# First pass of a one-core encoder block: more weight tiles between an operation and its use, open stage borders, plain fp32 for two of three query weights

## The chip, the cores and the metric

The kernel runs on one core of a Trainium2 chip. The metric is the device time of one execution in microseconds (us). Before the change its median is 3540.93 us over 3 runs (3540.81 to 3542.72). All times below are in us unless marked ns.

## The reference

One layer over 512 tokens of width 2048, in float32:

```
h    = rms_norm(x) * g1
q, k, v, f, pin, gates = split(h @ w_in)            # w_in: 2048 x 8200
attn = forgetting attention (8 heads of 128, causal, logits + cumsum(log_sigmoid(f)))
pool = (trailing means over 2/4/8/16 tokens - pin) @ w_groups * scale
y    = sig(g_a) * (attn @ w_branch_attn) + sig(g_p) * (pool @ w_branch_pool)
x    = x + y @ w_out
q2   = rms_norm(x) * g2 @ w_query                   # 8 heads x 256
idx, gate = top 16 of (q2a . keys1) + (q2b . keys2) per head, softmax
x    = x + sum_k gelu(xn . expert_u[idx]) * gate * expert_v[idx]
```

## The kernel before

The first 128 tokens (block A) go through the layer alone, in a **first pass**. The other 384 tokens follow in a second pass, and the experts after that. The change touches the first pass, and the point where the second begins.

**Weight tiles.** The first pass multiplies 112 weight tiles of 128 x 2048 (1 MB each), in the order of the list `plan` (L112 to L115): 0 to 63 for the projection (16 groups of 4: pin, pin, q, k, v, g, g, q, k, v, then six g), 64 to 79 for the branch projections, 80 to 95 for the output projection (wo), 96 to 111 for the query weights (wqu). "Tile 17" below is the one at place 17. Four tiles in a row make one 512-column result in PSUM.

**Two ways to use a tile.** A *split* tile is cut into two fp32r parts in two halves: ScalarE (ACT) casts the high part (`whi`, L162), VectorE (DVE) subtracts for the low part (`wlo`, L174), and TensorE (PE) does three matmuls for each of four k blocks. A *plain* tile (`None` in the plan) is used as it was loaded, in full fp32, four matmuls. Before the change every third tile is plain (place n with n % 3 == 2). Loads are issued by the SP queue (L152) into 3 buffers `wraw`, with a fourth (`xraw`) until near the end of the branch projections. A buffer comes free when the second `wlo` has read it, or for a plain tile when PE has multiplied it. `next_w`, `ahead` and `after` (L184 to L196) decide how far the loads and splits are issued ahead: some two tiles.

**Side work.** Everything else (pooling, head norms, attention of block A, the merge, the norm, the scores) is written as generators. In the middle of each tile's matmuls (L238) `run_gens` lets every live generator go on to its next `yield`, so one `yield` is one tile. What a generator issues to PE stands in PE's queue in the middle of that tile, and PE works through its queue in order, as every engine does. `qkA_norm` scales and squares four heads on ACT, takes a reciprocal root by Ln and Exp (L318, L319), multiplies on DVE (L478) and, one tile later, transposes on PE (L482). `attendA` does scores, softmax (L515 to L519), transposes (L523) and the product with v (L529). `mergedA` transposes the merged result (L591) and splits it, `normedA` does this for the new x (L657). `inputs_b` prepares the second pass's input: for each of 8 chunks it loads `xB` (L628) into one of two buffers, scales it (L636), casts (L638) and subtracts (`hl`, L640). The load of chunk c+1 stands in SP's queue right after the `hl` that frees its buffer was issued, among the loads of the weight tiles.

**Borders.** Before the branch projections all generators are run to their end (L571), before the output projection two rounds of them are run (L611), and after the query weights all of them (L880), which includes the retrieval's top 16 (`topk16`) of the last heads. Then the second pass starts with tile 112 and on.

Of the kernel before, what the change touches and what calls it, by code (L numbers as in the profile page):

```python
# [62 lines left out]
def block_kernel(ctx, tc, a):  # L63
# [48 lines left out]
    plan = [(a["w1A"][col1[kind] + i, q], "dve") for kind, i in groups_a for q in range(4)]  # L112
    for name in ("wbrA", "woA", "wquA"):
        plan += [(a[name][i, q], "dve") for i in range(4) for q in range(4)]
    plan = [(ap, None if n % 3 == 2 else eng) for n, (ap, eng) in enumerate(plan)]  # L115
    plan += [(a[src1[kind]][i], "dve") for kind, i in order_b]
    for name in ("wbr", "wo", "wqu"):
        plan += [(a[name][i], "dve") for i in range(KD)]
# [9 lines left out]
    cnt = [0]  # L128
# [3 lines left out]
    raws, his, parts = {}, {}, {}  # L132
# [33 lines left out]
    def ensure_split(n):  # L166

        ensure_hi(n)
        while st["split"] < min(n + 1, st["hi"]):
# [9 lines left out]
            else:  # L179
                parts[i] = (hi, lo)  # L180

    def next_w():
        n = st["use"]
        st["use"] += 1  # L184
        ensure_split(cnt[n + 1] - 1)
        ensure_load(n + (2 if extra["raws"] is None else 3))
        ensure_split(cnt[n] + 3)
        return parts.pop(n) if plan[n][1] else raws.pop(n)

    def ahead():  # L190
        n = st["use"]
        ensure_hi(cnt[n] + (2 if plan[n - 1][1] else 3))

    def after():
        n = st["use"]
        ensure_split(cnt[n] + (2 if plan[n - 1][1] else 3))  # L196

    gens = []

# [182 lines left out]
    def poolA(c, ps):  # L382
        t = rowsA(ps, "raw", 3)
        yield
        pm, pc = bank(), bank()
        for j in range(4):
            nc.tensor.matmul(pm[:, j * P:(j + 1) * P], lhsT=t[:, j * P:(j + 1) * P],
                             rhs=bands[:, 2 * c + j // 2, :], start=True, stop=True)
        for j in range(4):
            nc.tensor.matmul(pc[:, j * 16:(j + 1) * 16], lhsT=t[:, j * P:(j + 1) * P],  # L390
                             rhs=ident[:, P - 16:], start=True, stop=True)
        m = p1.tile([P, 4, NA], F32, name="mx", bufs=2)
        nc.scalar.copy(m.rearrange("p j t -> p (j t)"), pm)
        nc.scalar.copy(carry[:, 4 * c:4 * c + 4, :].rearrange("p j t -> p (j t)"), pc[:, :64])
        yield
        pg = bank()
        for gg in range(2):
            for dt in range(2):
                for kc in range(2):
                    o = (4 * c + 2 * gg + kc) * 256 + dt * P  # L400
                    i = 2 * gg + dt
                    nc.tensor.matmul(pg[:, i * P:(i + 1) * P], lhsT=wpgA[:, o:o + P],
                                     rhs=m[:, 2 * gg + kc, :], start=kc == 0, stop=kc == 1)
        for j in range(4):
            i = 4 * c + j
            nc.scalar.activation(ap32[:, 8 + i, :], pg[:, j * P:(j + 1) * P], AF.Copy,
                                 scale=psc[:, i:i + 1])
        split_to(ap32, aph, apl, 8 + 4 * c)
# [25 lines left out]
    def forgetA():  # L434
        yield
        ps = bank()
        for k in range(KD):
            nc.tensor.matmul(ps[:, :H], lhsT=xA[:, k, :], rhs=fraw[:, k * H:(k + 1) * H],
                             start=k == 0, stop=k == KD - 1)
        fl = p1.tile([P, H], F32, name="fr")  # L440
        nc.scalar.activation(fl, ps[:, :H], AF.Copy, scale=rsn[:, 0:1])
        yield
        pt = bank()
        nc.tensor.transpose(pt[:H, :NA], fl, ident)
        log_forget(p1, pt, NA, 0, ccA, 0.0, ("fz", "fe", "fu", "fl"))
        yield
        yield
        pt = bank()
        nc.tensor.transpose(pt[:, :H], ccA, ident[:H, :H])
        nc.scalar.copy(cT[:, 0, :], pt[:, :H])  # L450
# [17 lines left out]
    def qkA_norm(which, hb, ps):  # L468
        t = rowsA(ps, "raw", 3)
        v = p1.tile([P, 12], F32, name="hv", bufs=2)  # L470
        sq = p1.tile([P, S], F32, name="sqA")
        for j in range(4):
            nc.scalar.activation(sq[:, j * P:(j + 1) * P], t[:, j * P:(j + 1) * P], AF.Square,
                                 accum_out=v[:, j:j + 1])
        nc.vector.tensor_scalar(v[:, :4], v[:, :4], 1.0 / P, EPS, op0=OP.mult, op1=OP.add)
        rsqrt_nr(v[:, 4:8], v[:, :4], v[:, 8:])
        yield
        nc.vector.tensor_tensor(quad(t), quad(t), v[:, 4:8, None].to_broadcast([P, 4, P]), op=OP.mult)  # L478
        yield
        pt = bank()  # L480
        for j in range(4):
            nc.tensor.transpose(pt[:, j * P:(j + 1) * P], t[:, j * P:(j + 1) * P], ident)  # L482
        out = p1.tile([P, 4, NA], F32, name="n%d" % which)
        nc.scalar.activation(out.rearrange("p j t -> p (j t)"), pt, AF.Copy,
                             scale=(kg if which else qg)[:, 0:1])
        qkA[which, hb] = out
        if which:
            nc.scalar.dma_start(kA_d[hb], out)

    def attendA(hb, ps):  # L490
# [4 lines left out]
        for j in range(4):  # L495
            h = 4 * hb + j
            nc.sync.dma_start(ck[:, j, :], c_d[h:h + 1, :NA].to_broadcast([P, NA]))
        yield
        yield
        qn, kn = qkA.pop((0, hb)), qkA.pop((1, hb))  # L500
        pss = bank()
        for j in range(4):
# [15 lines left out]
        nc.vector.reciprocal(sm[:, :, 1:2], sm[:, :, 1:2])  # L518
        nc.vector.tensor_tensor(pr, pr, sm[:, :, 1:2].to_broadcast([P, 4, NA]), op=OP.mult)  # L519
        yield  # L520
        pt = bank()
        for j in range(4):
            nc.tensor.transpose(pt[:, j * P:(j + 1) * P], pr[:, j, :], ident)  # L523
        PT = p1.tile([P, 4, NA], F32, name="PT")
        nc.scalar.copy(PT.rearrange("p j t -> p (j t)"), pt)
        yield
        pa = bank()
        for j in range(4):
# [18 lines left out]
    for n, (kind, i) in enumerate(groups_a):  # L547
# [20 lines left out]
        after()  # L568
        if n == 9:
            gens.append(rest_rstd())  # L570
    for g in list(gens):  # L571
        for _ in g:
            pass
    gens.clear()
    es_1.close()


    mAh = pA.tile([P, KD, NA], F32R, name="XH")
    mAl = pA.tile([P, KD, NA], F32R, name="XL")
# [5 lines left out]
        yield  # L585

    def mergedA(i, ga):
        yield
        tb = bank()
        for j in range(4):  # L590
            nc.tensor.transpose(tb[:, j * P:(j + 1) * P], ga[:, j * P:(j + 1) * P], ident)  # L591
        nc.scalar.copy(m32[:, 4 * i:4 * i + 4, :].rearrange("p j t -> p (j t)"), tb)
        split_to(m32, mAh, mAl, 4 * i)

    for i in range(4):
# [12 lines left out]
        nc.vector.tensor_tensor(ga, ga, gb, op=OP.add)  # L608
        after()
        gens.append(mergedA(i, ga))  # L610
    for _ in range(2):  # L611
        run_gens()
    es_z.close()


# [6 lines left out]
    def inputs_b():  # L622
        rb = row_bcast(p2, [rsn[:, b:b + 1] for b in range(1, NTB)], "rstdB")
        xs = {}

        def load(c):
            xs[c] = p2.tile([P, 2, NB], F32, name="xB", bufs=2)
            nc.sync.dma_start(xs[c].rearrange("p j t -> p (j t)"), a["xB"][c])  # L628

        load(0)  # L630
        for c in range(KD // 2):
            if c + 1 < KD // 2:
                load(c + 1)
            for j in range(2):
                k = 2 * c + j
                nc.vector.scalar_tensor_tensor(xs[c][:, j, :], xs[c][:, j, :], g1[:, k:k + 1], rb,  # L636
                                               op0=OP.mult, op1=OP.mult)
                nc.scalar.copy(hh[:, k, :], xs[c][:, j, :])  # L638
                yield
                nc.vector.tensor_tensor(hl[:, k, :], xs[c][:, j, :], hh[:, k, :].bitcast(F32),  # L640
                                        op=OP.subtract)


    gens.append(inputs_b())
    nAh = pA.tile([P, KD, NA], F32R, name="YH")
# [5 lines left out]
    def normedA(i):  # L651
        xs = xr0[:, i * S:(i + 1) * S]
        nc.scalar.dma_start(x2t_d[:, i * S:(i + 1) * S], xs)
        yield
        tb = bank()
        for j in range(4):
            nc.tensor.transpose(tb[:, j * P:(j + 1) * P], xs[:, j * P:(j + 1) * P], ident)  # L657
        nc.vector.tensor_tensor(n32[:, 4 * i:4 * i + 4, :], quad(tb),
                                g2[:, 4 * i:4 * i + 4, None].to_broadcast([P, 4, NA]), op=OP.mult)
        split_to(n32, nAh, nAl, 4 * i)  # L660
        yield
        t = p3.tile([P, S], F32, name="scr", bufs=2)
        nc.scalar.activation(t, xs, AF.Square, accum_out=ssA[:, i:i + 1])

    for i in range(4):
        ps = acc_bank()
        for q in range(4):
            mmA(ps, m32, mAh, mAl, 4 * q, q == 0, q == 3, run_gens)
            ahead()
            if q < 3:  # L670
                after()
        xs = xr0[:, i * S:(i + 1) * S]
        nc.vector.tensor_tensor(xs, xs, ps, op=OP.add)
        after()
# [173 lines left out]
    def scores_a(c, ps, kk):  # L848
# [15 lines left out]
        s = pk.tile([P, 4, P], F32, name="s4", bufs=2)  # L864
        nc.scalar.activation(s.rearrange("p j t -> p (j t)"), pss, AF.Copy, scale=rstA[:, 0:1])
        yield
        for j in range(2):
            yield from blkA.job(2 * c + j, (s[:, 2 * j, :], s[:, 2 * j + 1, :]))

    for i in range(4):  # L870
        kk = p3.tile([P, 2, 2 * P], F32, name="kk", bufs=2)
        nc.scalar.dma_start(kk, a["keys"][2 * i:2 * i + 2].rearrange("h p i k -> p h (i k)"))
# [4 lines left out]
            after()  # L877
        gens.append(scores_a(i, ps, kk))
        run_gens_last()
    while gens:  # L880
        run_gens()

    es_y = [None]

    def start_rows():
        yield from tok_u(x2t_d, rstA[:, 0:1])
        for _ in blkA.decode():
            yield
# [685 lines left out]
```

## Time and profile before

| what | value |
|---|---|
| median of 3 runs | 3540.93 us |
| profiled execution | 3543.57 us |
| its span (first to last instruction) | 3541.8 us |
| PE busy over the span | 3353.7 us, 95% |
| DVE busy | 2699.1 us, 76% |
| ACT busy | 1525.5 us, 43% |
| granted clock of PE, mean | 0.976 |

The span is cut into stretches, and in each the idle time of PE and what ended it is read. A granted clock of 1.00 is the 2.4 GHz level, and time at 0.5 is the 1.2 GHz level, so 0.89 over a stretch means that 22% of it was at the lower level.

### The profile page before, as it was taken

Reading aid. Unit: us, or ns where it says so; the run is one execution under the profiler, and the core shown is the slowest. Engines: PE = TensorE matmul, PEld = TensorE weight load, DVE = VectorE, ACT = ScalarE, POOL = GpSimd, SP = SyncE. Lnnn points to the kernel's source line nnn. Section 1 sums busy time; section 2 is a strip of 40 time slices with the busy share of each in tenths; the row PEclk is TensorE's granted clock in tenths of the full one; section 3 lists DMA queues with packets and bytes.
Section 4 is the critical chain, followed back from the end, with each engine's and each line's share of the span. In section 5 each row is a group of like instructions: output and inputs, shape, how many; then the busy total and the mean of one; then the engine's idle time right before and its main releaser. Section 6 shows DMA issues by size and latency. Waiting matters only on the chain.

```text
span 3541.8 us, 50558 instructions
## 1 busy us (share of the span) xinstructions
PE 3353.7 (95%) x20256; PEld 3173.5 (90%) x20256; DVE 2699.1 (76%) x3492; ACT 1525.5 (43%) x2273; POOL 628.7 (18%) x399
## 2 busy tenths in 40 slices
PE   7898689999998999999999998999998999999998
PEld 5555468999998999999999998999998999999997
DVE  4445587887876878797777776888887888888885
ACT  4555333545453433335557673333332333333332
POOL 0000002332322212220000001222222222222220
PEclk9899799999999999999999999999999999999999
DMA  6687566786867888884645579999998999899984
GB/s 249 260 322 296 219 245 240 274 316 266 317 265 269 344 331 327 298 301 142 218 169 188 204 259 363 344 356 355 342 358 305 379 355 348 339 355 343 359 339 155
DMA packets 228044, 1036.93 MB, mean 293 GB/s; under 512 B 21344, under 2 KB 108560, under 8 KB 114208
## 3 DMA queue, kind: packets, MB, share of 16 engines
q1 hardware_dynamic: 145792, 577.29, 43.1%
q0 software_dynamic: 55520, 402.77, 30.3%
q10 hardware_dynamic: 26496, 53.64, 4.0%
q8 instruction: 159, 2.61, 0.3%
q14 instruction: 77, 0.63, 0.0%
HBM read 980.05 MB, written 53.56 MB: 292 GB/s over the span
## 4 chain that ended last, share of the span: by engine, by line
PE 52%; issue 21%; DVE 13%; DMA 7%; ACT 6%; POOL 1%; ACTq 0%; SPq 0%; POOLq 0%; DVEq 0%
PE psv L218 8%; PE psv L219 8%; PE psv L217 7%; PE psm L219 7%; PE psm L217 7%; PE psm L218 7%; PE psm L236 5%; DVE wlo L174 4%; DVE tok L809 2%; DMA row<-v,gidx 2%; ACT whi L162 2%; DMA wraw<-w1A 1%; DMA wraw<-woA 1%; ACT h5h L1419 1%; PE psx L218 1%
## 5 line engine op out<-in xcount | busy, mean ns | idle before, releaser
L174 DVE TENSOR_TENSOR wlo<-wraw,whi 128x1024 fp32r<-128x1024 f32 x738 | 880.3, 1220 | 318.1 <-ACT whi L162 316.5
L162 ACT CAST whi<-wraw 128x1024 fp32r<-128x1024 f32 x738 | 763.6, 1047 | 698.7 <-PE psv L218 392.7
L219 PE MATMUL psv<-h5h,wlo 128*128 128x320 f32 x2048 | 636.8, 311 | 18.2 <-DVE wlo L174 18.2
L219 PE MATMUL psm<-xnh,wlo 128*128 128x320 f32 x2048 | 636.1, 311 | 10.9 <-DVE wlo L174 10.8
L217 PE MATMUL psm<-xnh,whi 128*128 128x320 f32 x2048 | 638.8, 312 | 7.2 <-ACT at L1387 6.7
L217 PE MATMUL psv<-h5h,whi 128*128 128x320 f32 x2048 | 637.1, 311 | 4.7 <-ACT h5h L1419 4.4
L218 PE MATMUL psv<-h5l,whi 128*128 128x320 f32 x2048 | 638.1, 312 | 1.0
L218 PE MATMUL psm<-xnl,whi 128*128 128x320 f32 x2048 | 634.9, 310 | 0.0
L769 POOL DMA_INDIRECT row<-v,gidx x140 | 221.7, 1584 | 1160.9 <-DVE tok L809 1100.3
L769 POOL DMA_INDIRECT row<-u,gidx x135 | 212.7, 1576 | 1118.2 <-DVE row L806 543.4
L219 PEld LDWEIGHTS psv<-h5h,wlo 128*128 128x128 f32 x2048 | 387.4, 189 | 19.5 <-DVE wlo L174 19.5
L219 PEld LDWEIGHTS psm<-xnh,wlo 128*128 128x128 f32 x2048 | 387.7, 189 | 12.8 <-DVE wlo L174 12.8
L217 PEld LDWEIGHTS psm<-xnh,whi 128*128 128x128 f32 x2048 | 387.9, 189 | 7.8 <-ACT at L1387 7.0
L217 PEld LDWEIGHTS psv<-h5h,whi 128*128 128x128 f32 x2048 | 387.6, 189 | 6.8 <-ACT h5h L1419 6.4
L218 PEld LDWEIGHTS psv<-h5l,whi 128*128 128x128 f32 x2048 | 387.4, 189 | 4.8 <-DVE h5l L1420 4.3
L218 PEld LDWEIGHTS psm<-xnl,whi 128*128 128x128 f32 x2048 | 387.8, 189 | 0.0
L217 PE MATMUL psm<-hh,whi 128*128 128x384 f32 x1024 | 353.6, 345 | 0.0
L219 PE MATMUL psm<-hh,wlo 128*128 128x384 f32 x1024 | 347.3, 339 | 4.3 <-DVE wlo L174 4.3
L218 PE MATMUL psm<-hl,whi 128*128 128x384 f32 x1024 | 346.4, 338 | 0.0
L809 DVE SCALAR_TENSOR_TENSOR tok<-row,gact,tok 128x2048 f32<-128x2048 f32 x140 | 328.3, 2345 | 15.2 <-DMA row<-v,gidx 14.3
L806 DVE SCALAR_TENSOR_TENSOR row<-row,tok 128x2048 f32<-128x2048 f32 x135 | 307.6, 2284 | 13.0 <-DMA row<-u,gidx 12.9
L162 ACT CAST whi<-xraw 128x1024 fp32r<-128x1024 f32 x148 | 153.6, 1046 | 178.9 <-PE psv L218 148.1
(391 smaller groups left out, 5204.2 us busy)
## 6 DMA issues: line engine op xcount, KB each, us to landing
wraw<-uT SPq DMA_DIRECT2D x112, 1024.0 KB, 6.7
wraw<-vd SPq DMA_DIRECT2D x96, 1024.0 KB, 7.6
wraw<-w1A SPq DMA_DIRECT2D x48, 1024.0 KB, 6.7
xraw<-vd SPq DMA_DIRECT2D x32, 1024.0 KB, 8.9
wraw<-wgl SPq DMA_DIRECT2D x23, 1024.0 KB, 9.4
g_d<-stg ACTq DMA_DIRECT2D x10, 2048.0 KB, 11.4
gt<-g_d SPq DMA_DIRECT2D x32, 640.0 KB, 11.0
xraw<-w1A SPq DMA_DIRECT2D x16, 1024.0 KB, 7.7
```

The costliest lines, as they stand in the source:

```text
L162: nc.scalar.copy(hi, raws[i][:, half * HD:(half + 1) * HD])
L174: nc.vector.tensor_tensor(lo, raws[i][:, half * HD:(half + 1) * HD], hi.bitcast(F32), op=OP.subtract)
L217: nc.tensor.matmul(ps, lhsT=wh, rhs=xh, start=first and i == 0, stop=False)
L218: nc.tensor.matmul(ps, lhsT=wh, rhs=xl, start=False, stop=False)
L219: nc.tensor.matmul(ps, lhsT=wl, rhs=xh, start=False, stop=last and i == n - 1)
L236: nc.tensor.matmul(ps, lhsT=xs[:, k, :], rhs=ws, start=first and kk == 0 and n == 0, stop=last and kk == 3 and n == len(terms) - 1)
L769: nc.gpsimd.indirect_dma_start(out=r, out_offset=None, in_=a[kind], in_offset=bass.IndirectOffsetOnAxis(ap=gidx[grp][:, j:j + 1], axis=0))
L806: nc.vector.scalar_tensor_tensor(r, r, 1.0, tok, op0=OP.mult, op1=OP.mult, accum_out=gact[:, j:j + 1])
L809: nc.vector.scalar_tensor_tensor(tok, r, gact[:, j:j + 1], tok, op0=OP.mult, op1=OP.add)
L1419: nc.scalar.copy(hp[0], at)
```

## The change

It moves `yield`s in (one to four more tiles before PE uses a result), drops the drains at the first two borders (three tiles of the output projection now run before the second drain), leaves only the last head group's retrieval open at the third, makes two of three query weight tiles plain, and limits how far ahead tiles are split.

```diff
-    plan = [(ap, None if n % 3 == 2 else eng) for n, (ap, eng) in enumerate(plan)]
+    plan = [(ap, None if (n % 3 == 2 if n < 96 else n % 3) else eng) for n, (ap, eng) in enumerate(plan)]
...
+    def near(n, target):
+
+        return min(target, cnt[min(n + (3 if extra["raws"] is None else 4), len(plan))] - 1)
...
-        ensure_split(cnt[n] + 3)
+        ensure_split(near(n, cnt[n] + 3))
...
     def poolA(c, ps):
         t = rowsA(ps, "raw", 3)
         yield
+        yield
...
         nc.vector.tensor_tensor(quad(t), quad(t), v[:, 4:8, None].to_broadcast([P, 4, P]), op=OP.mult)
-        yield
+        for _ in range(3):
+            yield
         pt = bank()
...
-        yield
-        yield
+        for _ in range(5):
+            yield
         qn, kn = qkA.pop((0, hb)), qkA.pop((1, hb))
...
         nc.vector.tensor_tensor(pr, pr, sm[:, :, 1:2].to_broadcast([P, 4, NA]), op=OP.mult)
         yield
+        yield
+        yield
...
-    for g in list(gens):
-        for _ in g:
-            pass
-    gens.clear()
-    es_1.close()
...
     def mergedA(i, ga):
         yield
+        yield
...
-    for _ in range(2):
-        run_gens()
+    def wo_tiles(ps, qs):
+        for q in qs:
+            mmA(ps, m32, mAh, mAl, 4 * q, q == 0, q == 3, run_gens)
+            ahead()
+            if q < 3:
+                after()
+
+    first_o = acc_bank()
+    wo_tiles(first_o, range(3))
+    for g in list(gens):
+        for _ in g:
+            pass
+    gens.clear()
+    es_1.close()
     es_z.close()
...
                 nc.scalar.copy(hh[:, k, :], xs[c][:, j, :])
                 yield
+                if j:
+                    yield
...
         nc.scalar.dma_start(x2t_d[:, i * S:(i + 1) * S], xs)
         yield
+        yield
...
         for j in range(2):
             yield from blkA.job(2 * c + j, (s[:, 2 * j, :], s[:, 2 * j + 1, :]))
+        chosen.append(c)
...
-    while gens:
+    while len(scored) < 4 or len(gens) > 1:
         run_gens()
...
     def start_rows():
+        while len(chosen) < 4:
+            yield
```

Three places show what the order of instructions becomes. The first is SP's queue in the output and query weights: `wraw<-woA` and `wraw<-wquA` are loads of weight tiles, `xB<-xB` those of the second pass's input. Before:

```order
L152 DMA wraw<-woA 128x2048 x3
L628 DMA xB<-xB 128x768 x2
L152 DMA wraw<-woA 128x2048 x2
L628 DMA xB<-xB 128x768
L152 DMA wraw<-woA 128x2048 x2
L628 DMA xB<-xB 128x768
L152 DMA wraw<-woA 128x2048 x2
L628 DMA xB<-xB 128x768
```

After, the same queue from the first `woA` load on:

```order
L152 DMA wraw<-woA 128x2048 x6
L648 DMA xB<-xB 128x768 x2
L152 DMA wraw<-woA 128x2048 x3
L648 DMA xB<-xB 128x768
L152 DMA wraw<-woA 128x2048 x3
L648 DMA xB<-xB 128x768
L152 DMA wraw<-woA 128x2048 x3
L648 DMA xB<-xB 128x768
```

Six tiles instead of three are loaded ahead of the first `xB`, and three instead of two between one `xB` and the next; the `xB` loads still stand among them.

The second is ACT's queue around the border to the output projection: casts of weight halves (`whi<-wraw`), the copy and cast of the merged block (`row<-psx`, `XH<-row`), and the copy of the broadcast row (`rstdB<-psx`). Before, from the casts of tiles 81 and 82 on:

```order
L162 CAST whi<-wraw 128x1024 x3
L592 COPY row<-psx 128x512
L412 CAST XH<-row 128x512
L162 CAST whi<-wraw 128x1024
L338 COPY rstdB<-psx 128x384
L638 CAST hh<-xB 128x384 x2
L162 CAST whi<-wraw 128x1024 x2
```

After, from the same casts on:

```order
L162 CAST whi<-wraw 128x1024 x6
L598 COPY row<-psx 128x512
L418 CAST XH<-row 128x512
L162 CAST whi<-wraw 128x1024 x2
L342 COPY rstdB<-psx 128x384
L658 CAST hh<-xB 128x384
```

The copy of the last merged block has moved behind the casts of tiles 81, 82 and 84, and the broadcast row behind those of tile 85.

The third is ACT's queue where the first query result leaves PSUM (`scr<-psm`), before PE transposes it. Before, from the casts of tiles 100 and 102 on:

```order
L162 CAST whi<-wraw 128x1024 x3
L850 COPY scr<-psm 128x512
L872 DMA kk<-keys 128x2x256
L162 CAST whi<-wraw 128x1024
L318 ACT_TABLE_LOAD
L318 ACTIVATE rstA<-ssA 128x1
```

After, from the casts of tile 102 on:

```order
L162 CAST whi<-wraw 128x1024 x2
L868 COPY scr<-psm 128x512
L893 DMA kk<-keys 128x2x256
L322 ACT_TABLE_LOAD
L322 ACTIVATE rstA<-ssA 128x1
```

The copy now waits behind both casts of tile 102, the second next split tile, where it stood behind one.

## Rows read from the trace of the kernel before

**Rows 1.** The page: PE's busy share in 40 slices of the span, tenths.

```profile
PE   7898689999998999999999998999998999999998
```

**Rows 2.** Busy time by stretch: PE, PEld, DVE, ACT, POOL, granted clock, DMA share, GB/s.

```profile
29.17:227.83 198.66, 169.38 (x636) 115.46 (x635) 93.53 (x133) 102.92 (x169) 0.00 (x0) 0.89 0.67 261
227.83:272.26 44.43, 44.43 (x161) 30.11 (x160) 22.54 (x23) 26.40 (x31) 0.00 (x0) 1.00 0.86 337
276.00:321.00 45.00, 44.89 (x170) 30.49 (x169) 29.67 (x31) 26.56 (x33) 0.00 (x0) 1.00 0.83 327
321.00:454.50 133.50, 91.34 (x285) 58.83 (x283) 66.53 (x88) 51.06 (x71) 0.00 (x0) 0.82 0.60 226
452.40:519.10 66.70, 54.69 (x234) 41.11 (x232) 59.29 (x224) 27.57 (x36) 0.00 (x0) 0.95 0.64 247
```

**Rows 3.** What PE waited for, 0 to 540 us: total, times, longest.

```profile
PE psx L657 <- DVE xr L673: 25.2, 4, 8.0
PE psx L482 <- DVE raw L478: 19.9, 4, 7.9
PE psx L856 <- ACT scr L850: 8.5, 4, 3.5
PE psx L523 <- DVE prA L519: 4.7, 2, 3.6
```

**Rows 4.** PE's timeline, two plain tiles (start, length; three more lie between).

```profile
227.83 3.59 PE L236 MATMUL psm<-xraw,xA 128*128 128x512 f32 x8
...
263.37 3.60 PE L236 MATMUL psm<-xraw,xA 128*128 128x512 f32 x8
```

**Rows 5.** PE's side matmuls (tile psx) alone in the projection stretch: busy, clock.

```profile
29.17:227.83 198.66, 22.16 (x154) 0.89 0.67 261
```

**Rows 6.** Timelines of ACT, DVE and PE around a head norm, in tile 33.

```profile
162.28 1.28 ACT L318 ACT_TABLE_LOAD   x1
163.80 1.28 ACT L319 ACT_TABLE_LOAD   x1
165.80 2.36 DVE L174 TENSOR_TENSOR wlo<-wraw,whi 128x1024 fp32r<-128x1024 f32 x2
168.91 1.09 PE L482 MATMUL psx<-ident,raw 128*128 128x128 f32 x4 [7.91 <-DVE raw L478]
```

**Rows 7.** DMA, 0 to 500 us, GB/s in 40 slices, and the token rows' loads.

```profile
GB/s 291 304 273 233 292 128 204 273 146 344 300 279 326 210 225 169 423 341 317 351 349 375 327 384 330 241 206 210 236 181 220 199 200 286 296 244 232 258 304 290
...
row<-x SPq DMA_DIRECT2D x3, 1024.0 KB, 12.4
```

**Rows 8.** PE's timeline at the border to the output projection.

```profile
334.16 1.09 PE L591 MATMUL psx<-ident,zA 128*128 128x128 f32 x4 [6.54 <-DVE zA L608]
```

**Rows 9.** The chain that ended last: one wait for a tile's load.

```profile
141.85 4.78 DMA wraw<-w1A
```

**Rows 10.** Timelines of SP, ACT and DVE over one round of the output stage.

```profile
360.86 0.88 SPq L152 DMA_DIRECT2D wraw<-woA  x2
372.72 1.98 ACT L162 CAST whi<-wraw 128x1024 fp32r<-128x1024 f32 x2
373.78 2.36 DVE L174 TENSOR_TENSOR wlo<-wraw,whi 128x1024 fp32r<-128x1024 f32 x2 [2.14 <-ACT whi L162]
376.06 0.55 DVE L640 TENSOR_TENSOR hl<-xB,hh 128x384 fp32r<-128x384 f32 x1
376.67 0.33 SPq L628 DMA_DIRECT2D xB<-xB  x1
```

**Rows 11.** SP's timeline by line: all loads of `xB` (ns, first and last start).

```profile
L628 SPq DMA_DIRECT2D xB<-xB x8: 327/328/425, 335.3 to 415.8; - x8
```

**Rows 12.** ACT's timeline: the cast ahead of the first query result's copy.

```profile
448.70 1.05 ACT L162 CAST whi<-wraw 128x1024 fp32r<-128x1024 f32 x1 [6.28 <-DMA wraw<-wquA]
```

**Rows 13.** DVE's timeline: second split half of tile 102, of tile 113 (first of x3).

```profile
451.21 1.22 DVE L174 TENSOR_TENSOR wlo<-wraw,whi 128x1024 fp32r<-128x1024 f32 x1 [0.20 <-ACT whi L162]
517.84 3.49 DVE L174 TENSOR_TENSOR wlo<-wraw,whi 128x1024 fp32r<-128x1024 f32 x3
```

More of the change, by code (lines that the diff above doesn't have):

```diff
@@ L191, in ahead @@
         n = st["use"]
-        ensure_hi(cnt[n] + (2 if plan[n - 1][1] else 3))
+        ensure_hi(near(n, cnt[n] + (2 if plan[n - 1][1] else 3)))
     def after():
         n = st["use"]
-        ensure_split(cnt[n] + (2 if plan[n - 1][1] else 3))
+        ensure_split(near(n, cnt[n] + (2 if plan[n - 1][1] else 3)))
     gens = []
@@ L445, in forgetA @@
         log_forget(p1, pt, NA, 0, ccA, 0.0, ("fz", "fe", "fu", "fl"))
-        yield
-        yield
+        for _ in range(6):
+            yield
         pt = bank()
@@ L497, in attendA @@
             nc.sync.dma_start(ck[:, j, :], c_d[h:h + 1, :NA].to_broadcast([P, NA]))
-        yield
-        yield
+        for _ in range(5):
+            yield
         qn, kn = qkA.pop((0, hb)), qkA.pop((1, hb))
@@ L587, in mergedA @@
     def mergedA(i, ga):
+        yield
         yield
@@ L639, in inputs_b @@
                 yield
+                if j:
+                    yield
                 nc.vector.tensor_tensor(hl[:, k, :], xs[c][:, j, :], hh[:, k, :].bitcast(F32),
@@ L654, in normedA @@
         yield
+        yield
         tb = bank()
@@ L665, in block_kernel @@
     for i in range(4):
[L666 to L671, printed above, removed]
+        ps = acc_bank() if i else first_o
+        wo_tiles(ps, range(4) if i else (3,))
         xs = xr0[:, i * S:(i + 1) * S]
@@ L866, in scores_a @@
         yield
+        scored.append(c)
         for j in range(2):
             yield from blkA.job(2 * c + j, (s[:, 2 * j, :], s[:, 2 * j + 1, :]))
+        chosen.append(c)
+    scored, chosen = [], []
     for i in range(4):
@@ L885, in start_rows @@
     def start_rows():
+        while len(chosen) < 4:
+            yield
         yield from tok_u(x2t_d, rstA[:, 0:1])
```

## The prediction

> **What bounds the kernel now.** I read the page first, for where PE idles; then a table by stretch, for how much; then the waits, for who is late; then timelines, for why.
>
> On the page PE's row of slices dips only in the first seventh of the span [rows 1]; after it every slice but four is at 90% or more, and those at 80%. So the second pass and the experts are PE's own work, and whatever the first pass gains arrives at the end of the program. The table splits the first pass into three parts [rows 2].
>
> *Projection (29.17 to 227.83, 45 tiles).* PE is busy 169.38 of 198.66, at a clock of 0.89. What it would take without stalls comes from the stretch behind it, where PE is never idle: four triples of tiles in 227.83 to 263.37 [rows 4], 8.885 a triple, 2.96 a tile. A plain tile lasts 3.59 from first to last matmul; I take 0.16 as lying beside the next tile, which leaves 3.43, and (8.885 - 3.43)/2 = 2.73 for a split one. So 45 tiles want 45 x 2.96 + 22.2 of side matmuls [rows 5] = 155.5, and 198.66 - 155.5 = 43.2 are lost: 29.3 idle, and 13.9 because PE worked at the 1.2 GHz level after idling. The wait list gives causes [rows 3]: 19.9 in four waits of the head norms' transposes for DVE, 4.7 for the softmax. The transposes stand one tile behind the multiplication that they need.
>
> *Output projection and first query weights (321 to 454.5).* PE is busy 91.34 of 133.50. The waits name the norm's transposes (25.2) [rows 3], but I take the loop of loads as the real limit. A round [rows 10]: an `xB` load on SP lets the next tile loads go at 360.86; the later one's cast starts at 372.72, its `wlo` follows, behind it on DVE stands the `hl` that frees the `xB` buffer, and at 376.67 SP may issue the next `xB`, with the next tiles behind it. A lone tile takes 4.78 to land [rows 9], a second one in line about 2.8 more (1 MB at some 375 GB/s, near the best slices of [rows 7]), `xB` 1.1, issue 0.4, and cast to `xB` issue 376.67 - 372.72 = 3.95: 13.0 for a round of two tiles. Measured: (415.8 - 335.3)/6 = 13.4 [rows 11]. PE needs 5.9 for two tiles, so it waits whatever is done on PE.
>
> *Later query weights and start of the second pass (452.4 to 519.1).* DVE is busy 59.29 of 66.70 [rows 2]: splits, `hl`, retrieval. This part is DVE's.
>
> **The change part by part.** *More yields in the projection.* No instruction comes or goes. A yield is a tile of 2.96, so two more put a head norm's transposes 5.9 later, which covers three of the four L482 waits; the attention ones, 3.6 and under, go. Something else is late next. In tile 33 [rows 6] PE stopped at 168.91 - 7.91 = 161.00. Without the stop it ends the tile about 1.4 later, and 0.5 into tile 34 (162.9) needs a `wlo` that starts at 165.80 and has its first half at 167.0, because DVE stood waiting on the rsqrt chain: 4.1 remain. For the next longest head norm I take 4.1 x 5.0/7.9 = 2.6, by the mean of the four waits over the longest. The three loads of token rows [rows 7] share the queue with 12 tiles: 15 MB (15.7 in decimal) at 350 GB/s are 44.9, against PE's 12 x 2.96 + 22.2 x 12/45 = 41.4, so 3.5 more of waiting (none at the 423 of one slice; 6.7 if no side work falls there). Together 10.2 idle, and half-speed time in proportion, 13.9 x 10.2/29.3 = 4.8. Gain: 43.2 - 15.0 = 28. Bounds: nothing left, 43; every wait changing hands, about 0; below zero only if ACT or DVE became full, and they are busy 103 and 94 of 199 [rows 2].
>
> The two table loads of 1.28 in each rsqrt chain lie in that 4.1 [rows 6]. The Trainium skill, "ScalarE: Activation LUTs", section "Table sets: the hidden batching unit", says that Ln followed by Exp needs one load, since one set holds both. The trace disagrees, with a load ahead of each; by the rule the remaining waits would be 1.28 shorter in each of the two norms and the sum 2.6 better. I keep the trace.
>
> *Borders left open.* The first drain has nothing left to do in before. At the second, PE's 6.54 for the merged block [rows 8] lies beside the loads of tiles 81 to 83, which must land anyway; its end lets the first `xB` go, at 335.3. After, ACT has the copy of the block behind the casts of tiles 82 and 84, three tiles more are issued ahead of the first `xB`, and I take that `xB` at the same time, 336, give or take 5.
>
> *The loop, three tiles a round.* From SP's order: x2, then six more `xB`, three tiles between each. A round is 13.0 + 2.8 = 15.8, still above PE's 8.9. Six rounds end at 336 + 95 = 431, and they now carry tiles 86 to 103 instead of 84 to 95. The `wlo` of tile 102 ends some 0.5 before the last `xB`, at 430.3; before it ended at 452.43 [rows 13]. Gain 22. Bounds: three tiles at the DMA rate, a gain of 54 (first rival); rounds of 17.5, 12. The norm's transposes, a tile later, wait less, but behind this loop that is worth nothing of its own.
>
> *Two of three query weights plain.* Five tiles become plain: 5 x 0.70 = 3.6 more of PE, and 5 x 2.36 less on DVE, 5 x 1.98 less on ACT. Up to tile 102 the loop covers the PE part. In the DVE-bound part (from `wlo` of 102 to that of 113) three splits go, 7.1, and 5.2 more of the input's work falls there (two `hl` at 0.55 [rows 10] and their scaling at some 2 each, an estimate): DVE 59.3 - 7.1 + 5.2 = 57.4, with the same 7.4 of waits 64.8. Gain 2. The first `scr` copy stands behind both casts of tile 102 now, so PE's L856 waits (8.5 in all, [rows 3]) get longer, on an engine that is not the bound there. If that cover is gone it costs what the third rival says.
>
> *Third border, `near`, the rest.* One retrieval goes on while tiles 112 to 119 run; it is DVE work beside DVE work, and the row gathers behind it shift by a tile. `near` changes nothing where one of three is plain. I cost these at nothing, with 3 either way.
>
> Sum: 28 + 22 + 2 = 52 or 53 off the profiled 3543.57, which is 2.6 above the median; against the median 3540.93 it gives 3488.
>
> **Rivals.** *The loads stream.* If `hl` is done while tiles are in flight, the round is DMA's: 3.54 MB at 337 GB/s is 10.5, not 15.8, and 5.3 x 6 = 32 more go: 3456. For it: 276 to 321 runs with PE busy 44.89 of 45.00 with the same kind of tiles [rows 2]. Against: that stretch has a fourth buffer and no `xB` in the queue. The Trainium skill, "DMA: Bandwidth & Descriptors", section "Specifications", gives some 358 GB/s for a core's HBM share; one slice shows 423 [rows 7], so the trace does not bear it as a cap. By it the round would be 9.9 and the time 3452.
>
> *The waits change hands.* Every head norm keeps the 4.1 that I worked out for tile 33 (16.4 in all), both softmax waits half of theirs (2.4), the token rows 3.5: 22.3 idle, 10.6 at half speed, a gain of 10; and the rounds take 17.5, as the slower half of before's did more than the mean: 12, and 2. Time 3517. For it: DVE and ACT work in order, and a moved PE wait frees neither. Against: rounds of before agree with the sum to 0.4.
>
> *The score copies bind (slower).* Each of four groups' `scr` copy waits behind both casts of the tile after next. Before, the one cast ahead of it had waited 6.28 for its load [rows 12]; with both, 6.28 + 1.98 = 8.3. If PE, not DVE, sets the end there, 4 x 8.3 = 33, 3.6 for the plain tiles and 7.4 at the second border (its 6.54, and 0.9 more) are paid and the loop's gain is lost: 44 against 28, time 3557. It decides from the point where tile 102's load lands more than about 7 after PE has finished tile 99; loads in threes make that less likely, not more.
>
> *The change does nothing to the end.* The row gathers, not PE, could set when the experts begin, and the early tiles would be waited out there: 3541. Against it stand the full slices after the first pass [rows 1].
>
> **How the numbers follow.** Forecast 0.57 (its own range 3466 to 3506: the projection's residual between 5 and 25, the start of the loop 5 either way, rounds 15 to 17), streaming loads 0.14, waits change hands 0.20, score copies 0.05, nothing 0.04. Predicted time 3488. The range goes from 3453 to 3520, which leaves out the last two rivals and the tails. About 0.2% (7) is what a measurement tells from no change. Faster 0.91, same 0.04, slower 0.05.
>
> **What would show it.** In the profile after: the L482 waits under 2 each, and waits of L236 for `wlo` in tiles 18 and 34 in their stead; the clock of the projection near 0.96 with PE over 90% busy; six rounds between `xB` loads of 15 to 17; the `wlo` of tile 102 near 400 in the new trace (430 less 28); DVE busy about 57 from there to tile 113. Wrong would be: rounds of 11 (first rival), PE idle in L868's transposes with DVE idle too (third), or `whi` and load waits of the old size in the projection (second).

## The result, and the profile after

The changed kernel takes 3495.39 us (median of 4 runs, 3489.91 to 3495.98) against 3541.2 for before in the same comparison: 0.9866 of it, 95% interval [0.9849, 0.9883]. That is 46 faster; 52 or 53 were forecast (3488). The profiled execution is 48.5 shorter in its span (3541.8 to 3493.3).

The page's row of PE by slices answers [rows 1]:

```profile
PE   7999799999998999999999998999999999999998
```

Of the five slices under 90% at the start, two are left: the first, and the fifth (349 to 437 us), which is the later output projection and the query weights. Roughly the same stretches as in [rows 2], as they lie after (columns as there; the third is from the `wlo` of tile 102 to that of tile 113):

```profile
26.00:199.00 173.00, 163.34 (x643) 112.75 (x642) 90.81 (x134) 100.33 (x168) 0.00 (x0) 0.96 0.79 304
300.00:405.00 105.00, 76.39 (x242) 45.67 (x241) 53.32 (x69) 39.95 (x55) 0.00 (x0) 0.89 0.67 253
405.02:476.09 71.07, 61.93 (x227) 42.14 (x226) 54.61 (x217) 23.86 (x34) 0.00 (x0) 0.90 0.66 252
```

The projection is now PE's: 163.34 busy of 173.00, at a clock of 0.96 where it was 0.89. The first two stretches do not begin and end at the same tiles as before. By equal ends, PE's start of tile 2 to its start of tile 47 went from 198.66 to 166.49, and the load of tile 80 to the end of the `wlo` of tile 102 from 131.1 to 111.1. The third stretch is longer than it was, 71.07 for 66.70, with less DVE work in it: 54.61 for 59.29, so DVE stands idle for 16.5 of it.

What PE waited for up to 540 us, seven of eleven entries, for [rows 3] (total, times, longest). Of the first one, 19.7 lie ahead of 30 us, where the program starts.

```profile
PE psm L240 <- ACT whi L162: 20.2, 4, 15.4
PE psm L240 <- DMA wraw<-woA: 11.5, 3, 5.0
PE psx L874 <- ACT scr L868: 9.4, 2, 5.5
PE psm L240 <- DVE wlo L174: 9.0, 7, 3.5
PE psx L880 <- ACT scr L876: 4.7, 2, 4.0
PE psm L240 <- ACT YH L418: 4.1, 1, 4.1
PE psm L240 <- DMA wraw<-w1A: 2.9, 1, 2.9
```

The waits of the side transposes for DVE are gone from the list, 25.2 for the norm and 19.9 for the head norms; of PE's waits for DVE in side matmuls, 1.3 is left for the broadcast row. What comes instead is the weights themselves: loads of the output projection, low parts, and copies behind casts (`scr` is a query result or its transpose, `YH` the high part of the new x). The three longest waits that remain in the projection stand in PE's timeline at tile 18, at tile 34 and among the loads of the token rows:

```profile
92.00 0.79 PE L240 MATMUL psm<-wlo,XH 128*128 128x512 f32 x1 [2.54 <-DVE wlo L174]
...
147.25 0.80 PE L240 MATMUL psm<-wlo,XH 128*128 128x512 f32 x1 [3.48 <-DVE wlo L174]
...
184.43 1.22 PE L240 MATMUL psm<-wraw,xA 128*128 128x512 f32 x1 [2.93 <-DMA wraw<-w1A]
```

The forecast had 2.6, 4.1 and 3.5 for these. ACT's timeline at tile 34 has the chain of the head norm, with its two table loads, between the first half's cast and the second's:

```profile
139.48 1.04 ACT L162 CAST whi<-wraw 128x1024 fp32r<-128x1024 f32 x1 [0.67 <-DMA wraw<-w1A]
...
142.44 1.28 ACT L322 ACT_TABLE_LOAD   x1
143.74 0.21 ACT L322 ACTIVATE hv<-hv 128x4 f32<-128x4 f32 x1
143.96 1.28 ACT L323 ACT_TABLE_LOAD   x1
145.26 0.20 ACT L323 ACTIVATE hv<-hv 128x4 f32<-128x4 f32 x1
145.37 1.98 ACT L162 CAST whi<-wraw 128x1024 fp32r<-128x1024 f32 x2
```

PE waits for the low part of the first half, whose cast was done at 140.52. It is late because DVE, in order, first waits for ACT's part of the chain:

```profile
145.49 0.17 DVE L324 SCALAR_TENSOR_TENSOR hv<-hv 128x4 f32<-128x4 f32 x1 [2.87 <-ACT hv L323]
...
145.97 2.36 DVE L174 TENSOR_TENSOR wlo<-wraw,whi 128x1024 fp32r<-128x1024 f32 x2
```

(The Trainium skill, "ScalarE: Activation LUTs", section "Table sets: the hidden batching unit", would have one load for Ln and Exp together; here too there are two.)

The loop of loads in the output stage, in SP's timeline, for [rows 10, 11]:

```profile
309.42 0.80 SPq L648 DMA_DIRECT2D xB<-xB  x2
332.47 0.33 SPq L648 DMA_DIRECT2D xB<-xB  x1
347.19 0.33 SPq L648 DMA_DIRECT2D xB<-xB  x1
363.61 0.33 SPq L648 DMA_DIRECT2D xB<-xB  x1
376.70 0.33 SPq L648 DMA_DIRECT2D xB<-xB  x1
393.32 0.33 SPq L648 DMA_DIRECT2D xB<-xB  x1
408.16 0.33 SPq L648 DMA_DIRECT2D xB<-xB  x1
```

Six rounds in 408.16 - 309.79 = 98.4, 16.4 a round; 15.8 was forecast. The waits of SP's queue between 300 and 405 us say whom it waits for:

```profile
SPq L648 <- DVE hl L662: 58.7, 5, 14.3
SPq L152 <- PE psm L240: 13.1, 5, 4.9
```

And DVE's timeline has the two ends of the last stretch, for [rows 13]: the `wlo` of tile 102 ends at 405.02 (452.43 before), the last half of tile 113 at 476.09 (519.06).

```profile
402.66 2.36 DVE L174 TENSOR_TENSOR wlo<-wraw,whi 128x1024 fp32r<-128x1024 f32 x2 [7.21 <-ACT whi L162]
...
474.87 1.22 DVE L174 TENSOR_TENSOR wlo<-wraw,whi 128x1024 fp32r<-128x1024 f32 x1
```

### The profile page after: what moved, and what is told of

It is laid out like the page before. It is cut to its first block, busy times and chain, and to the rows that moved or that the text cites. A ratio compares the mean times of both kernels' runs of the same rounds, so it can differ in the third digit from the quotient of the medians.

```text
span 3493.3 us, 50472 instructions
## 1 busy us (share of the span) xinstructions
PE 3344.0 (96%) x20236; PEld 3163.3 (91%) x20236; DVE 2685.3 (77%) x3482; ACT 1515.5 (43%) x2263; POOL 642.8 (18%) x399
## 4 chain that ended last, share of the span: by engine, by line
PE 62%; DVE 13%; issue 9%; DMA 7%; ACT 7%; POOL 1%; ACTq 0%; SPq 0%; POOLq 0%; DVEq 0%
PE psm L223 10%; PE psm L221 10%; PE psm L222 10%; PE psv L222 7%; PE psv L223 7%; PE psv L221 7%; PE psm L240 6%; DVE wlo L174 4%; DMA row<-v,gidx 3%; ACT whi L162 2%; DVE tok L827 1%; ACT o L1385 1%; PE psx L1366 1%; POOL row L787 1%; PE psx L222 1%
## 5 line engine op out<-in xcount | busy, mean ns | idle before, releaser
L174 DVE TENSOR_TENSOR wlo<-wraw,whi 128x1024 fp32r<-128x1024 f32 x728 | 869.5, 1220 | 321.3 <-ACT whi L162 319.5
L162 ACT CAST whi<-wraw 128x1024 fp32r<-128x1024 f32 x728 | 753.4, 1047 | 691.3 <-PE psv L222 368.0
L787 POOL DMA_INDIRECT row<-u,gidx x135 | 220.0, 1629 | 1092.4 <-DVE row L824 547.3
L824 DVE SCALAR_TENSOR_TENSOR row<-row,tok 128x2048 f32<-128x2048 f32 x135 | 307.5, 2285 | 15.2 <-DMA row<-u,gidx 15.2
```

The source lines that it names most:

```text
L162: nc.scalar.copy(hi, raws[i][:, half * HD:(half + 1) * HD])
L174: nc.vector.tensor_tensor(lo, raws[i][:, half * HD:(half + 1) * HD], hi.bitcast(F32), op=OP.subtract)
L787: nc.gpsimd.indirect_dma_start(out=r, out_offset=None, in_=a[kind], in_offset=bass.IndirectOffsetOnAxis(ap=gidx[grp][:, j:j + 1], axis=0))
L824: nc.vector.scalar_tensor_tensor(r, r, 1.0, tok, op0=OP.mult, op1=OP.mult, accum_out=gact[:, j:j + 1])
```

## The experiments

Since the parts of the change are worth 0 to 27 us, and single runs of one kernel lie up to 14 apart, each profile was also cut in three by SP's loads. Up to the load of tile 80 is the projection and the branch projections; from there to the load of tile 116 (which waits for the `wlo` of 113) the output and query weights; the rest is the second pass and the experts. Except for `before`, `before_xb_pool`, `yields_only`, `no_yields`, `borders_closed` and the two `xb_chain` kernels, all have the same code in the first part as the changed kernel, and there they differ by up to 8.7. So the middle column is the one to read. It is the issue of tile 116's load less that of tile 80's in each trace. The ratio is to the runs of before that went with each kernel. The intervals of `four_a_round`, `wqu_third` and `third_closed` touch that of the changed kernel at their ends, though no run of theirs is as short as its longest (3495.98), so a price of 9 among these is not a sharp one.

| kernel | median | ratio to before, interval | load of tile 80 | 80 to 116 | 116 to end |
|---|---|---|---|---|---|
| before | 3541.2 | 1 | 321.3 | 197.8 | 3022.7 |
| changed | 3495.4 | 0.9866 [0.9849, 0.9883] | 293.9 | 182.2 | 3017.2 |
| yields_only | 3514.2 | 0.9922 [0.9905, 0.9938] | 297.4 | 198.6 | 3022.6 |
| no_yields | 3522.9 | 0.9951 [0.9935, 0.9968] | 318.6 | 186.2 | 3018.1 |
| two_a_round | 3496.0 | 0.9876 [0.986, 0.9893] | 295.1 | 184.2 | 3014.7 |
| four_a_round | 3504.9 | 0.9895 [0.9878, 0.9911] | 297.4 | 184.1 | 3021.6 |
| wqu_third | 3504.3 | 0.9897 [0.988, 0.9913] | 297.5 | 191.5 | 3014.8 |
| borders_closed | 3497.9 | 0.9883 [0.9866, 0.9899] | 297.0 | 184.6 | 3013.6 |
| third_closed | 3504.1 | 0.9898 [0.9881, 0.9914] | 298.3 | 187.3 | 3019.6 |
| before_xb_pool | 3511.1 | 0.9922 [0.9905, 0.9938] | 319.1 | 171.5 | 3018.7 |
| xb_pool | 3478.5 | 0.9821 [0.9803, 0.9839] | 295.7 | 165.4 | 3017.1 |
| xb_pool_third | 3474.8 | 0.9812 [0.9796, 0.9828] | 302.6 | 162.2 | 3017.1 |
| xb_chain | 3476.4 | 0.9817 [0.98, 0.9833] | 295.1 | 164.3 | 3015.3 |
| xb_chain_scr | 3473.1 | 0.981 [0.9794, 0.9827] | 290.1 | 163.1 | 3018.2 |

**The projection's yields: alone on before, and taken from the changed kernel.**

```diff
 # yields_only: before, with these yields and those of pooling, forget gate and
 # softmax, which are not printed; no_yields: the changed kernel without them
     def qkA_norm(which, hb, ps):
...
-        yield
+        for _ in range(3):
+            yield
...
     def attendA(hb, ps):
...
-        yield
-        yield
+        for _ in range(5):
+            yield
```

> The kernel before with the added yields of the projection alone (pooling, forget, head norm, attention); borders, query tiles and input preparation as before. Theory (the projection's gain stands by itself): the waits of L482 go, about 3.5 and 2.5 remain in tiles 34 and 18 for the low parts, tile 80's load goes out some 27 us earlier than before, and all of it arrives at the end: 3514 us (3508 to 3520). Rival (the gain needs the open borders, because the drain at the first border now finds generators to run out): under 20 us of gain, 3522 or more.

> The changed kernel without the added yields of the projection (pooling, forget, head norm, attention); the rest as changed. Theory (parts add up: these yields alone gave 26 us on the kernel before): 26 us slower, 3516 to 3527. Rival (the open borders and the later stages take up part of it): 3505 to 3514.

Measured: 3514.23 and 3522.88. One way the yields give about 26 (against the 3540.55 of before in that comparison), the other way 27.5, and nearly all of it by the load of tile 80 (23.9 and 24.7). These yields add to the rest; neither rival holds.

**Two, and four tiles to a round of the loop.**

```diff
 # two_a_round
                 yield
-                if j:
-                    yield
```
```diff
 # four_a_round
                 yield
-                if j:
-                    yield
+                yield
```

> The changed kernel without the second yield for every second k block of the input preparation, so that two tiles and not three stand between one xB load and the next. Theory (the loop of loads sets the output stage): rounds between xB loads fall from 16.4 to about 13.4 us but carry two tiles, and the time rises by some 22 us: 3517 us (3510 to 3525). Rival (the transposes of the norm set that stage, the xB loads only lie in it): no change within 5 us, 3490 to 3500.

> The changed kernel with one more yield per two k blocks of the input preparation, so four tiles instead of three between one xB load and the next. Theory of the prediction (a round costs 13.0 plus 2.8 per tile over two, so more tiles a round is cheaper per tile): rounds of about 18.6 us, some 5 to 8 us faster, 3487 to 3491. Rival formed on the run with two a round (what a longer loop gains by tile 102 is given back from there to tile 113, where DVE waits for splits behind the remaining rounds): no gain, 3493 to 3505, and the stretch from the wlo of tile 102 to that of 113 longer than 71 us.

Measured: 3496.03 with two, 3504.87 with four. The theory of the prediction fails in both; with four the rival came true. The rounds with two are as computed, those with four longer: 13.4 and 20.2 on average, where 13.4 and 18.6 were expected, by the first and last of eight `xB` loads in SP's timeline (two, then four):

```profile
L648 SPq DMA_DIRECT2D xB<-xB x8: 327/328/424, 311.3 to 392.0; - x8
```
```profile
L648 SPq DMA_DIRECT2D xB<-xB x8: 328/328/424, 313.8 to 435.6; - x8
```

But a loop with fewer tiles in a round is over sooner. With two a round the `wlo` of tile 102 ends at 416.68, 121.6 after the load of tile 80; with three 111.1 after; with four 103.9 after. From there to the `wlo` of tile 113 (first two, then four):

```profile
416.68:479.21 62.53, 56.84 (x226) 39.08 (x224) 50.05 (x208) 22.25 (x30) 0.00 (x0) 0.97 0.74 281
```
```profile
401.34:481.45 80.11, 60.58 (x226) 40.90 (x224) 60.25 (x232) 25.12 (x37) 0.00 (x0) 0.89 0.60 229
```

62.5, 71.1 and 80.1: what the third tile gains by tile 102, 10.5, it gives back but for some 2 by tile 113. The fourth gains 7.2 and gives back 9.0. In this stretch PE waits 3.5, 8.5 and 15.2 for the score copies, and none, five and eight of the sixteen `hl` fall there. Of what stands in the way the `xB` loads in SP's queue are not the main thing: `xb_pool`, below, has them elsewhere, and there the stretch is still this long, with five `hl` in it:

```profile
391.15:461.09 69.94, 59.05 (x226) 40.92 (x224) 54.52 (x218) 23.90 (x34) 0.54 (x1) 0.93 0.67 257
```

The longest of the waits for a copy in that stretch of the changed kernel shows a way. An input cast `hh<-xB` on ACT waits for DVE, which is at the top 16; the copy stands behind that cast, and PE waits for the copy:

```profile
427.70 0.51 ACT L658 CAST hh<-xB 128x384 fp32r<-128x384 f32 x1 [7.17 <-DVE xB L656]
428.12 0.58 ACT L876 COPY scr<-psx 128x512 f32<-128x512 f32 x1
...
428.75 1.26 PE L880 MATMUL psx<-kk,scr 128*128 128x128 f32 x8 [3.99 <-ACT scr L876]
```

That the input's work as a whole makes the stretch longer in this way is argued from these rows; no run takes it out alone. With four a round the input is also not done when the query weights end, so the rounds that drain it there run the last head's retrieval too: its first step stands at 477.21, ahead of the last `wlo` of tile 113, as in `third_closed` below. So the 9 of this kernel are not those of the loop alone.

**One of three query weight tiles plain, with the loop and without it.**

```diff
 # wqu_third; xb_pool_third has this and the next edit
-    plan = [(ap, None if (n % 3 == 2 if n < 96 else n % 3) else eng) for n, (ap, eng) in enumerate(plan)]
+    plan = [(ap, None if n % 3 == 2 else eng) for n, (ap, eng) in enumerate(plan)]
```
```diff
 # xb_pool: the changed kernel; before_xb_pool: the same on before
-            nc.sync.dma_start(xs[c].rearrange("p j t -> p (j t)"), a["xB"][c])
+            nc.gpsimd.dma_start(xs[c].rearrange("p j t -> p (j t)"), a["xB"][c])
```

> The changed kernel with one of three query weight tiles plain, as before. Theory of the prediction (DVE sets the later query weights, three splits fewer help it): slower by about 2 us, 3497 us. Rival formed on the trace of the changed kernel (a plain tile gives its buffer back only when PE has multiplied it, so loads wait for PE and splits for loads; DVE waits 16.5 of 71 us there): faster by 4 us or more, 3491 or less, DVE's waits from tile 102 to 113 back near 7 us.

> The changed kernel with the xB loads issued on POOL's queue instead of SP's, so that no weight load stands behind an xB load. Theory (the loop of loads sets the output stage: the weight loads wait in SP's queue for hl): PE's waits in 300 to 405 us, 28.6 us now, fall by more than half, and the time falls by 15 to 35 us: 3460 to 3480. Rival (the weight loads are late for another reason, such as buffers held until a split or PE is done, or the norm's chain): within 5 us of 3495.

> The xB loads on POOL's queue and one of three query weight tiles plain, as before. The run with one of three plain and the loads on SP was 9 us slower than the changed kernel, where 2 were forecast. Theory (the second split tile of a round lengthens the loop of xB loads by its cast and subtraction, so most of the 9 us go with the loop): 2 to 4 us slower than the POOL version's 3478, 3478 to 3484. Rival (the plain tiles relieve DVE and ACT whatever the queue): still 8 us or more slower, 3486 or more.

> The kernel before with the xB loads alone on POOL's queue. Theory (the loop of loads was the limit of the output stage before too): 15 to 25 us faster than before, 3516 to 3526. Rival (the transposes of the norm, 25.2 us of waits by the trace, were the limit): within 5 us of before, 3536 to 3546.

Measured: `wqu_third` 3504.27, 9 slower, 9.3 by the middle column. The sign was the prediction's, the size not, and the rival (faster) is wrong. SP's timeline of this kernel shows the place, the rounds over tiles 95 to 103:

```profile
368.63 0.33 SPq L648 DMA_DIRECT2D xB<-xB  x1
383.56 0.33 SPq L648 DMA_DIRECT2D xB<-xB  x1
402.86 0.33 SPq L648 DMA_DIRECT2D xB<-xB  x1
421.42 0.33 SPq L648 DMA_DIRECT2D xB<-xB  x1
```

14.9, 19.3 and 18.6, where the changed kernel has 13.1, 16.6 and 14.8: with two split tiles among three, one more cast and subtraction stand ahead of the `hl`. `xb_pool_third` bears it out: without the loop one of three plain is no worse than two of three (3474.82 and 3478.49, intervals overlapping).

`xb_pool` took 3478.49, 17 less, and `before_xb_pool` 3511.08, 29 less than before; 15 to 35 and 15 to 25 were expected. PE's waits between 300 and 405 us fell from 28.6 to 14.3, half and not more than half. So the loop of loads was the limit of the output stage in both kernels, and the rival of the transposes falls: with the `xB` loads elsewhere the norm's waits shrink on the kernel before without any change to the norm, from 25.2 [rows 3] to

```profile
PE psx L657 <- DVE xr L673: 12.4, 4, 4.7
```

and in `xb_pool` SP no longer waits for `hl` but for what frees the weight buffers, PE and the splits:

```profile
SPq L152 <- PE psm L240: 42.1, 11, 5.8
SPq L152 <- DVE wlo L174: 26.4, 10, 3.8
```

**The borders.**

```diff
 # borders_closed
+    for g in list(gens):
+        for _ in g:
+            pass
+    gens.clear()
+    es_1.close()
     mAh = pA.tile([P, KD, NA], F32R, name="XH")
...
-    first_o = acc_bank()
-    wo_tiles(first_o, range(3))
-    for g in list(gens):
-        for _ in g:
-            pass
-    gens.clear()
-    es_1.close()
+    for _ in range(3):
+        run_gens()
...
```
```diff
 # third_closed
-    while len(scored) < 4 or len(gens) > 1:
+    while gens:
         run_gens()
...
-        while len(chosen) < 4:
-            yield
```

> The changed kernel with the first two borders drained as before (all generators run out before the branch projections, three rounds of them before the output projection), yields and query tiles as changed. Theory of the prediction (the borders are covered by the loads): within 5 us of the changed kernel, 3490 to 3500. Rival (PE's wait of about 7 us for the last merged block is on the path again, with half-speed time behind it): 3502 to 3510.

> The changed kernel with the third border drained as before (the last heads' retrieval ends before tile 112 is used). Theory of the prediction (retrieval is DVE work beside DVE work): within 3 us of the changed kernel, 3492 to 3498. Rival (PE waits out the last top 16, some 8 us of DVE): 3502 or more.

Measured: 3497.9 for the first two borders, which agrees with their price of nothing: PE waits 8.0 for the merged block again, and the time does not show it. Inside the middle part it does show: three tiles fewer are loaded ahead of the first `xB`, and by the `wlo` of tile 102 this kernel is 9.4 behind (120.5 for 111.1 from the load of tile 80), of which it has 7.1 back by tile 113 (64.0 for 71.1). The third border is another matter: 3504.14, 9 slower, where the rival had 3502 or more; 5.1 of it lie in the middle part and 2.4 after it in the profiles. DVE's timeline in `third_closed`, where the second half of tile 113 is split (`cf` is the first step of a head's top 16), and PE's next row:

```profile
481.25 0.42 DVE L736 TENSOR_TENSOR cf<-v,v 128x256 f32<-128x256 f32 x1
484.28 2.35 DVE L174 TENSOR_TENSOR wlo<-wraw,whi 128x1024 fp32r<-128x1024 f32 x2
```
```profile
485.55 0.69 PE L223 MATMUL psm<-hh,wlo 128*128 128x384 f32 x1 [3.34 <-DVE wlo L174]
```

In the changed kernel the last head's `cf` stands behind that `wlo` and not ahead of it, and PE waits 0.7 there:

```profile
476.01 0.42 DVE L736 TENSOR_TENSOR cf<-v,v 128x256 f32<-128x256 f32 x1
```

The retrieval of one head takes 5.2 (from the `cf` at 476.07 to that at 481.25 in `third_closed`). The waiting PE then works at the 1.2 GHz level for a while: in 480 to 500 us its clock is 0.83 and it is busy 16.7, where the changed kernel has 1.00 and 19.3 in 470.6 to 490.6. The stretch from the load of tile 116 to that of tile 140 is 220.8 long with 219.1 of PE work in the one, and 216.5 with 214.9 in the other.

**What is left.** Two more on top of `xb_pool`:

```diff
 # xb_chain: the reciprocal root's DVE part a tile later (the helper written out)
-        rsqrt_nr(v[:, 4:8], v[:, :4], v[:, 8:])
-        yield
+        out, tmp, vv = v[:, 4:8], v[:, 8:], v[:, :4]
+        nc.scalar.activation(out, vv, AF.Ln)
+        nc.scalar.activation(out, out, AF.Exp, scale=-0.5)
+        yield
+        nc.vector.scalar_tensor_tensor(tmp, out, -0.5, out, op0=OP.mult, op1=OP.mult)
+        nc.vector.tensor_tensor(tmp, tmp, vv, op=OP.mult)
+        nc.vector.scalar_tensor_tensor(out, tmp, 1.5, out, op0=OP.add, op1=OP.mult)
         nc.vector.tensor_tensor(quad(t), quad(t), v[:, 4:8, None].to_broadcast([P, 4, P]), op=OP.mult)
```
```diff
 # xb_chain_scr: that, and the scores' copy ahead of the next casts
             mmA(ps, n32, nAh, nAl, 4 * q, q == 0, q == 3, run_gens)
-            ahead()
-            after()
+            if q < 3:
+                ahead()
+                after()
         gens.append(scores_a(i, ps, kk))
         run_gens_last()
+        ahead()
+        after()
```

> The xB loads on POOL's queue, and in the head norms DVE's part of the reciprocal root one tile later, so that the wlo of tiles 18 and 34 does not stand behind ACT's Ln and Exp. Theory (DVE's wait for the chain is what is left): the waits of 2.5 and 3.5 us there go, with some half-speed time, 3 to 7 us faster than the POOL version's 3478: 3471 to 3476. Rival (the second cast of those tiles stands behind the chain on ACT as well): waits of 1 us or more remain and the time is the same, 3476 to 3483.

> As the last one, and after the fourth tile of each query group the copy of the result out of PSUM is issued ahead of the casts of the next tiles. Theory (PE's waits of 7.1 us for that copy in the later query weights come from the casts ahead of it on ACT): they fall under 2 us in all, 4 to 8 us faster than the one without: 3465 to 3471. Rival (the casts, now behind the copy, make the low parts late instead): no gain, waits of L240 or L223 for wlo or whi of 4 us or more.

Measured: 3476.36 and 3473.13; intervals overlap with `xb_pool` and with each other, so neither theory is shown. By the traces both half hold. The first frees tile 18, and in tile 34 a wait of 1.4 for the cast is left, as its rival had it. The second takes the copy's wait from 7.0 to 3.0, but that of the next copy, which the edit does not move, goes from 5.1 to 8.1, and the `wlo` of the second pass costs 3.2:

```profile
PE psx L885 <- ACT scr L881: 8.1, 3, 4.4
PE psm L223 <- DVE wlo L174: 3.2, 1, 3.2
```

Both beat the changed kernel; so do `xb_pool` and `xb_pool_third`, by 17 to 22, and which of these four is best the runs can't tell.

## Why the prediction was nearly right, point by point

The time, the range and the direction held. Of the sum of 28, 22 and 2 only the first came about as it was argued.

- *Projection, 28.* Right in size and cause: 27.4 by the load of tile 80 in the profile, 26 and 27.5 by the two experiments, and the three waits that were to be left (2.6, 4.1, 3.5) are there with 2.54, 3.48 and 2.93, at the places named. One thing was not foreseen: tiles 2 to 47 themselves gained 32.2, and 4.2 of it went back in the nine tiles behind (30.9 for 26.7), where the last matmuls of the attention (1.7) and waits of 1.4 now fall.
- *The loop as the limit.* Right for before and after: moving the `xB` loads to another queue takes 29 from the one and 17 from the other, and the rounds of two and three tiles agree with the sum on average (13.4 for 13.0, 16.4 for 15.8); single rounds of before lie between 11.7 and 16.2.
- *Three tiles a round, 22.* This is the step that failed. "Six rounds end at 336 + 95 = 431, and they now carry tiles 86 to 103" came about: by tile 102 the changed kernel is indeed 20 ahead beyond the projection's gain (47.4 - 27.4). But I took what is gained by tile 102 as gained at the end; from the load of tile 80 to that of tile 116, 24 were forecast and 15.6 came (197.8 to 182.2). Taken out alone the third tile in a round is worth 10.5 of it, the plain tiles 6.4 (with one of three it is 117.5 and not 111.1 from the load of tile 80 to there), and the three tiles more ahead of the first `xB`, which came with the open border, 9.4; these overlap, since their sum is more than 20. And the stretch behind, to tile 113, which I took as 2 shorter, is 4.4 longer. It is not DVE's, as I had it: DVE is idle for 16.5 of its 71.07, and PE waits 8.5 there for score copies and works at a clock of 0.90. With two tiles a round it is 62.5. The third tile is worth 0.6 in the medians and 2 in the middle part.
- *Plain query tiles, 2.* The step "Up to tile 102 the loop covers the PE part" looked at PE alone. In the loop it is the second split of a round that lies on the path, so five fewer splits gave 9. From tile 102 to tile 113 the gain alone is near what I said, 73.9 with one of three plain and 71.1 with two of three, but its terms are not: five `hl` fall there and not two, and a scaling takes 0.61 and not 2.
- *The third border, nothing with 3 either way.* Mis-sized: 9 by the medians, 7.5 in the profile behind tile 80. "DVE work beside DVE work" left out that PE waits for the split that stands behind the last retrieval (3.3), and works at half speed for part of the time behind it.
- *First two borders, nothing.* Right at the end within what can be measured (2.5); the 9.4 by tile 102 are given back like the third tile's.

Taken one at a time from the changed kernel the parts are worth 27, 9, 9, 2.5 and 0.6, in sum 48 against the 46 measured. `near` and the yields in the merge and the norm were not taken out alone, and since the parts overlap by tile 102 the sum does not show that each of these is nothing. The nearness of 3488 to 3495 is in part luck: a term of 22 that was really about 1 to 2, and two of 2 and 0 that were 9 each.

Of the rivals, streaming loads did not happen, since `hl` still held the `xB` loads (58.7 of SP's waiting). The waits did change hands in the output stage, to loads that stand behind `xB`, but not in the projection. The score copies do bind at single places (5.5 and 3.9), and not at all four.

What stays open: where the up to 8.7 between runs of equal code ahead of tile 80 come from (some 4 are there before PE starts tile 11, at 64.9 to 69.4); what makes the stretch from tile 102 to tile 113 longer, beyond the rows shown; and part of the 5.5 that the changed kernel gains behind the load of tile 116. Of these, 3.0 lie ahead of the load of tile 140, where the third border shows, and the rest is within what kernels with the same code behind that load differ by.

## What to carry to other kernels

A wait in an in-order queue is paid by all that stands behind it. Here an input load that waited for DVE in the weights' queue cost both kernels more than most of the change's parts gave; asking which queue an unrelated load waits in comes before spacing the work that waits. When a loop with a fixed number of rounds is to carry more work per round, work out the time to the end of the last stretch that shares its engines, not to the end of the loop: what is gained early may be given back where the loop now reaches. And a sum that comes out right proves no term of it; only taking each part out alone did.

## What was not expected of the hardware

Runs of one kernel differ more here than the three runs of before had shown (3540.81 to 3542.72): four runs of `xb_pool_third` lie between 3469.59 and 3483.71, and among profiles with the same code ahead of it the load of tile 80 lies between 293.9 and 302.6. So parts worth 2 or 3 us can't be told by medians of four runs here, and inside a trace only where their own rows show them.
